# Streamed tiles spaced 64 bytes apart in a pool of their own, a reordered first unit, and last columns in halves

## The chip, the cores and the metric

The kernel runs on one core of a Trainium2 chip. The metric is the device time of one execution in microseconds (us). Three runs of the kernel before gave 2600.47, 2601.5 and 2602.29 us; the median is 2601.5 us.

## The reference

Two decoder layers over 256 tokens of width 2048, all in float32. Each layer adds three things to the residual x: a mixer, a cross-attention and a gated feed-forward block, each behind an RMS norm. The mixer projects the normed x to 6924 columns and runs four attention variants of four heads each side by side.

```python
for layer in range(DEPTH):                       # 2
    h = rms_norm(x, mix_norm[layer])
    proj = h @ w_in[layer]                       # 2048 x 6924
    ...                                          # retention, stick-breaking, hgrn2, nsa
    x = x + mix @ w_out[layer]                   # 2048 x 2048
    x = x + cross_attention(rms_norm(x, ..), rms_norm(mem, ..), ..)
    x = x + conv_ffn(rms_norm(x, ..), ffn_w_up[layer], .., ffn_w_down[layer])   # 2048 x 11264, 5632 x 2048
return rms_norm(x, final_norm)
```

Nearly all the arithmetic is the product of 256 rows of activations with weights that are read once.

## The kernel before, in words

The weights come as 880 units in one fixed list. A unit is a slab of up to 128 x 1024 float32 values: two slices of 128 rows of K by 512 columns (`group_a`), or four slices by 256 columns (`group_b`). For each unit one DMA on SP's queue fills a tile `raw` (`u_dma`, L392), ScalarE copies it into a tile `hi` of the narrower type float32r (`u_hi`, L397), and VectorE writes the remainder raw - hi into a tile `lo` (`u_lo`, through the helper at L247). Activations lie in the same form: `xt_tile` gives a tile of 128 x 2 x 256 whose first half holds the high part (`hi_part`, by `act` at L242 or a copy at L260) and whose second half the low part (`lo_part`, L247 or L250). A tag `xt` holds normed inputs, a tag `mg` the outputs of the attention variants and of the gated block; 16 buffers each.

Every product is three matmuls: high by high, high by low, low by high. `group_a` holds an activation tile stationary and streams 512 columns of weight (L411, L412, L413, moving `hi`, `lo`, `hi`). `group_b` holds 128 weight columns stationary and streams the activation tile: eight matmuls of 512 columns (L476, moving both halves of `xt`, stationary `hi`) and eight of 256 columns (L479, stationary `lo`).

One pool `sb` holds every tile in order of first use. The tags `xt`, `hi` and `lo` follow one another in buffers of 2048 or 4096 bytes per partition, so all their tiles start at the same place within every 512 bytes. Between `lo` and `mg` lie small tiles of 17088 bytes in all, 33 times 512 and 192 more, so each `mg` tile starts 192 bytes further within 512 than a `hi` or `lo` tile.

The main loop walks the units. At unit i it issues the DMA of unit i + 6, does `more(i)` (loads of x, constants and parameters at fixed units), makes `hi` of unit i + 3 and `lo` of unit i + 2, then issues the unit's matmuls and one step of each side chain (`tick`). Before the loop the first six units are loaded, with the four transposed pieces of x (`turned`) in between, and `first_norm` makes the first activation tiles. Each engine works through its instructions in program order.

At the end `group_tail` (L432) computes the last 512 columns: the last three units first for token rows 0 to 127, then for rows 128 to 255, and `last_rows` (L1469) adds each half to x, takes the sum of squares, forms 1/sqrt by `rsqrt` (L497: logarithm, exponential and one Newton step), scales four tiles and stores them from SP's queue (L1491).

Of the kernel before, what the change touches and what calls it, by code (L numbers as in the profile page):

```python
# [133 lines left out]
def shape_consts():  # L134
    f = np.float32
    i = np.arange(128)
    c = {}
    lg = np.log1p(-np.exp2(-5.0 - np.arange(H)))
    rel = (i[None, :] - i[:, None]).astype(np.float64)
    dec = np.zeros((128, H, 2, 128))  # L140
    for h in range(H):
        dec[:, h, 0] = np.where(rel >= 0, np.exp(lg[h] * np.maximum(rel, 0)), 0.0)
        dec[:, h, 1] = np.exp(lg[h] * (rel + 128))
    ident = np.eye(128)
    ones = np.ones((128, 128))
# [12 lines left out]
    inv = (10000.0 ** (-(np.arange(64) / 64))).astype(f)  # L158
    half_pi = np.full((128, 1), np.pi / 2)
    parts = [("ident", ident), ("ones", ones), ("inv", np.broadcast_to(inv, (128, 64))), ("hpi", half_pi),  # L160
             ("tri", tri), ("dec", dec * SCALE), ("sbm", sbm), ("cm", cm),
             ("sel", (i[:, None] % 32 == np.arange(15)[None, :]) * 1.0), ("cadd", np.where(ok, 0.0, NEG)), ("cmul", ok * 1.0)]
# [31 lines left out]
def body(ctx, tc, w, x, xt_in, mem, mem_t, pos, consts, masks, pars, wck, wcv, fnorm, out):  # L194
# [5 lines left out]

    sb = ctx.enter_context(tc.tile_pool(name="sb", bufs=1))
# [3 lines left out]
    count = [0]  # L205

# [16 lines left out]
    def xt_tile(tag):  # L223
        return sb.tile([128, 2, 256], F32R, name=nm(tag), tag=tag, bufs=16)
# [76 lines left out]
    nc.sync.dma_start(par[0][:, 0:16], pars[0, :, 0:16])  # L301
# [10 lines left out]
    def more(i):  # L312

        if i in (1, 3, 5, 7):
            k = i // 2
            for t in range(2):
                nc.sync.dma_start(xs[t][k], x[t * 128:(t + 1) * 128, k * 512:(k + 1) * 512])
        elif i == 6:
# [18 lines left out]
    stage = {}  # L337
# [50 lines left out]

    def u_dma(u):
        n = u.nk * u.cols  # L390
        u.raw = sb.tile([128, n], F32, name=nm("raw"), tag="raw", bufs=AHEAD - LO + 1, padded_shape=[128, 1024])
        nc.sync.dma_start(u.raw, bass.AP(tensor=w.tensor, offset=u.off, ap=[[n, 128], [1, n]]))  # L392

    def u_hi(u):
        n = u.nk * u.cols
        u.hi = sb.tile([128, n], F32R, name=nm("hi"), tag="hi", bufs=HI + 1, padded_shape=[128, 1024])
        A.copy(u.hi, u.raw)  # L397

    def u_lo(u):
        n = u.nk * u.cols  # L400
        u.lo = sb.tile([128, n], F32R, name=nm("lo"), tag="lo", bufs=LO + 1, padded_shape=[128, 1024])
        tt(u.lo, u.raw, f(u.hi), OP.subtract)
        u.raw = None
# [28 lines left out]
    def group_tail(src, klists, n, ends):  # L432
# [3 lines left out]
        late = []  # L436

        def products(u, kl, i, rows):
            for j, k in enumerate(kl):
                mm_a(u, st["ps"], src(k), j, n, i == 0 and j == 0, i == z and j == len(kl) - 1, rows)  # L440

        for i, kl in enumerate(klists):
            def pe(u, i=i, kl=kl):
                if i == 0:
                    st["ps"] = [acc([128, 512]) for _ in range(2)]
                if i < z - LO:
                    products(u, kl, i, (0, 1))
                elif i == z - LO:
                    late.extend((units[u.at + d], klists[i + d], i + d) for d in range(LO + 1))
                    late[:] = [(v, v.hi, v.lo, a, b) for v, a, b in late]  # L450
                    for v, _, _, a, b in late:
                        products(v, a, b, (0,))
                else:
                    for v, hi, lo, a, b in late:
                        v.hi, v.lo = hi, lo
                        products(v, a, b, (1,))
                    del late[:]

            def done(i=i):
                start(ends[i == z](st["ps"][i == z]))  # L460
            unit(pe, done if i in (z - LO, z) else None,
# [179 lines left out]
    def layer(l):  # L641
# [791 lines left out]
        for what, g, k in ffn_order():  # L1433
# [4 lines left out]
            elif what == "down" and g[-1] == tail[-1] and k == 3 and nn is None:  # L1438
                group_tail(gsrc, pairs(g), 512, (last_rows(0), last_rows(1)))
# [9 lines left out]
    def last_chunk(k):  # L1449
        def ev(ps):  # L1450
# [12 lines left out]
            yield  # L1463
# [5 lines left out]
    def last_rows(t):  # L1469

        def ev(ps):
            n = fin["n"]
            tt(xs[t][3], xs[t][3], ps, OP.add)
            n.squares(3, (t,))
            tot = small(1)
            V.tensor_reduce(tot, n.ss[:, t], axis=AX.X, op=OP.add)  # L1476
            steps = rsqrt(tot, 1, 1.0 / D)
            while True:
                try:
                    next(steps)  # L1480
                except StopIteration as e:
                    r = e.value
                    break
            for q in range(4):
                if q % 2 == 0:
                    act(xs[t][q], xs[t][q], AF.Copy, scale=r[:, 0:1])
                elif q == 1:
                    ts(xs[t][q], xs[t][q], r[:, 0:1], None, OP.mult)
                else:
                    stt(xs[t][q], xs[t][q], r[:, 0:1], fin["g"][q], OP.mult, OP.mult)  # L1490
                nc.sync.dma_start(out[t * 128:(t + 1) * 128, q * 512:(q + 1) * 512], xs[t][q])  # L1491
            yield from ()
        return ev
# [12 lines left out]
    def first_norm():  # L1506
        n = NORM[0]
        for k in range(4):
            yield from n.chunk_of(k, xT.pop(k))
        for k in range(4):  # L1510
            yield
# [15 lines left out]
    first = first_norm()  # L1527
    next(first)
    u_hi(units[0])
    u_hi(units[1])  # L1530
    next(first)
    start(first)
    u_hi(units[2])
    for i in range(LO):
        u_lo(units[i])
    for i in range(n):
        if i + AHEAD < n:
            u_dma(units[i + AHEAD])
        more(i)
        if i + HI < n:  # L1540
# [81 lines left out]
```

## Time and profile before

| | |
|---|---|
| Median of three runs | 2601.5 us |
| The profiled execution's own time | 2601.13 us |
| Its span, first to last instruction | 2599.3 us |
| PE (TensorE matmul) busy | 2577.4 us, 99% |
| PEld (weight load) busy | 2211.7 us, 85% |
| DVE (VectorE) busy | 1777.1 us, 68% |
| ACT (ScalarE) busy | 1364.5 us, 52% |
| DMA queue of SP | 54.9% of 16 engines' span |
| Mean granted TensorE clock | 0.999 |

Busy time of PE is not the same as PE at its peak: matmuls are pipelined, and each record reaches from the start of one matmul to a modelled end that lies inside the next one. What a matmul costs in a dense stream is the distance from its start to the start of the next, and that is read from the timeline. A line such as L247 is that of a helper and stands for many places of the program; the tile names tell them apart.

### The profile page before, as it was taken

How to read it: one execution, taken by the hardware profiler on the slowest of the kernel's cores; microseconds unless marked ns; L12 is line 12 of the kernel's file. 1: busy time of each engine (PE TensorE's matmuls, PEld its weight loads, DVE VectorE, ACT ScalarE, POOL GpSimd, SP SyncE). 2: the span in 40 equal slices, each digit the busy share in tenths (PEclk: the TensorE clock that was granted, in tenths of full speed). 3: DMA queues.
4: the chain of work that ended last, by engine and by line, in shares of the span. 5: the costliest groups of instructions: out<-in, count | busy, mean ns of one | idle time of the engine just before them, and what ended most of it. 6: DMA issues, size and time to landing. Idle time of an engine off the chain costs nothing. (4 is left out here: it accounts for less than half of the span.)

```text
span 2599.3 us, 37253 instructions
## 1 busy us (share of the span) xinstructions
PE 2577.4 (99%) x13842; PEld 2211.7 (85%) x13842; DVE 1777.1 (68%) x2877; ACT 1364.5 (52%) x2157; POOL 45.5 (2%) x79
## 2 busy tenths in 40 slices
PE   8999999999999999999999999999999999999998
PEld 7888888888888888888889888889888888888886
DVE  6776665667667676676768666656676766766766
ACT  6545545566455555454555455445654545454554
POOL 0010000000000000000000100000000000000000
PEclk9999999999999999999999999999999999999999
DMA  7564466545555555655555744655455555656654
GB/s 275 180 228 139 153 199 217 188 153 188 188 187 192 189 192 186 193 182 193 186 181 161 227 135 151 205 183 180 159 188 191 189 189 188 191 188 192 205 189 142
DMA packets 136439, 483.66 MB, mean 186 GB/s; under 512 B 15937, under 2 KB 16449, under 8 KB 136257
## 3 DMA queue, kind: packets, MB, share of 16 engines
q1 hardware_dynamic: 131456, 465.55, 54.9%
q0 software_dynamic: 4800, 15.73, 1.9%
q8 instruction: 109, 1.79, 0.3%
q14 instruction: 74, 0.60, 0.1%
HBM read 479.12 MB, written 2.10 MB: 185 GB/s over the span
## 5 line engine op out<-in xcount | busy, mean ns | idle before, releaser
L247 DVE TENSOR_TENSOR lo<-raw,hi 128x1024 fp32r<-128x1024 f32 (+2 forms) x880 | 1067.7, 1214 | 752.6 <-issue 281.3
L397 ACT CAST hi<-raw 128x1024 fp32r<-128x1024 f32 (+2 forms) x880 | 917.8, 1044 | 1174.8 <-PE acc L413 506.2
L476 PE MATMUL acc<-xt,hi 128*128 128x512 f32 x3456 | 870.6, 394 | 9.0 <-ACT hi L397 9.0
L476 PEld LDWEIGHTS acc<-xt,hi 128*128 128x128 f32 x3456 | 623.4, 189 | 125.3 <-ACT hi L397 9.0
L479 PEld LDWEIGHTS acc<-xt,lo 128*128 128x128 f32 x3456 | 471.5, 190 | 33.9
L479 PE MATMUL acc<-xt,lo 128*128 128x256 f32 x3456 | 481.8, 282 | 0.0
L411 PE MATMUL acc<-hi,mg 128*128 128x512 f32 (+1 forms) x1152 | 439.6, 382 | 0.1
L413 PE MATMUL acc<-hi,mg 128*128 128x512 f32 (+1 forms) x1152 | 438.5, 381 | 0.0
L412 PE MATMUL acc<-lo,mg 128*128 128x512 f32 (+1 forms) x1152 | 436.5, 379 | 0.0
L412 PEld LDWEIGHTS acc<-lo,mg 128*128 128x128 f32 x1152 | 216.4, 188 | 42.8
L411 PE MATMUL acc<-hi,xt 128*128 128x512 f32 (+2 forms) x640 | 252.0, 394 | 0.0
L411 PEld LDWEIGHTS acc<-hi,mg 128*128 128x128 f32 x1152 | 216.5, 188 | 41.7 <-ACT mg L260 1.0
L413 PEld LDWEIGHTS acc<-hi,mg 128*128 128x128 f32 x1152 | 216.5, 188 | 40.9 <-DVE mg L247 0.3
L413 PE MATMUL acc<-hi,xt 128*128 128x512 f32 (+2 forms) x640 | 243.2, 380 | 0.0
L412 PE MATMUL acc<-lo,xt 128*128 128x512 f32 (+2 forms) x640 | 242.9, 380 | 0.0
L250 DVE SCALAR_TENSOR_TENSOR s<-s,par,s 128x255 f32<-128x255 f32 x352 | 161.9, 481 | 6.3
L411 PEld LDWEIGHTS acc<-hi,xt 128*128 128x128 f32 x640 | 120.4, 188 | 21.0 <-issue 2.3
L412 PEld LDWEIGHTS acc<-lo,xt 128*128 128x128 f32 x640 | 120.4, 188 | 20.8 <-issue 1.9
L413 PEld LDWEIGHTS acc<-hi,xt 128*128 128x128 f32 x640 | 120.1, 188 | 20.6
L242 ACT ACTIVATE s<-s,par 128x256 f32<-128x256 f32 x176 | 96.0, 593 | 0.6 <-DVE s L247 0.6
L247 DVE TENSOR_TENSOR s<-acc,s 128x256 f32<-128x256 f32 x224 | 83.9, 417 | 0.0
L247 DVE TENSOR_TENSOR x<-x,acc 128x512 f32<-128x512 f32 x128 | 81.9, 681 | 1.9 <-PE acc L413 1.9
(184 smaller groups left out, 1381.6 us busy)
## 6 DMA issues: line engine op xcount, KB each, us to landing
raw<-in_w_dram SPq DMA_DIRECT2D x848, 512.0 KB, 3.5
raw<-in_w_dram SPq DMA_DIRECT2D x16, 396.0 KB, 3.1
raw<-in_w_dram SPq DMA_DIRECT2D x16, 384.0 KB, 3.0
s<-in_nsa_w_ck_dram POOLq DMA_DIRECT2D x16, 256.0 KB, 5.6
s<-in_nsa_w_cv_dram POOLq DMA_DIRECT2D x16, 256.0 KB, 4.6
s<-in_memt_dram POOLq DMA_DIRECT2D x16, 256.0 KB, 5.0
s<-in_xt_dram SPq DMA_DIRECT2D x8, 256.0 KB, 6.4
x<-in_x_dram SPq DMA_DIRECT2D x8, 256.0 KB, 5.9
```

What stands on the lines that cost most here:

```text
L242: A.activation(o, i, func, bias=bias, scale=scale)
L247: V.tensor_tensor(o, a, b, op=op)
L250: V.scalar_tensor_tensor(o, a, s, b, op0=op0, op1=op1)
L397: A.copy(u.hi, u.raw)
L411: T.matmul(ps[t][:, 0:n], lhsT=xh, rhs=hi, start=first, stop=False)
L412: T.matmul(ps[t][:, 0:n], lhsT=xh, rhs=lo, start=False, stop=False)
L413: T.matmul(ps[t][:, 0:n], lhsT=xl, rhs=hi, start=False, stop=last)
L476: T.matmul(st["ps"][q].rearrange("p a b -> p (a b)"), lhsT=u.hi[:, at:at + 128], rhs=xk[kk].rearrange("p a b -> p (a b)"), start=i == 0 an ...
L479: T.matmul(st["ps"][q][:, 1, :], lhsT=u.lo[:, at:at + 128], rhs=xk[kk][:, 0, :], start=False, stop=i == 3 and kk == 3)
```

## The change

Three parts. First, `raw`, `hi`, `lo`, `xt` and `mg` move into a pool `flow` that is opened before `sb`, behind a filler of 1920 bytes; a tile of `hi` or `lo` takes 4160 bytes instead of 4096, one of `xt` or `mg` 2112 instead of 2048. Second, the first loads are put in order of need, the first unit's load, copy and remainder are done in two halves, and two loads go on ScalarE's queue. Third, the last 512 columns are computed in three parts (rows 0 to 127 whole, rows 128 to 255 in two halves of columns), the final scaling of a part is written behind the sum of the next, and `rsqrt` has fewer steps.

```diff
+    flow = ctx.enter_context(tc.tile_pool(name="flow", bufs=1))
     sb = ctx.enter_context(tc.tile_pool(name="sb", bufs=1))
...
+    flow.tile([128, 480], F32, name="edge", tag="edge")
...
     def xt_tile(tag):
-        return sb.tile([128, 2, 256], F32R, name=nm(tag), tag=tag, bufs=16)
+        o = flow.tile([128, 512], F32R, name=nm(tag), tag=tag, bufs=16, padded_shape=[128, 528])
+        return o.rearrange("p (a b) -> p a b", a=2)
...
-    nc.sync.dma_start(par[0][:, 0:16], pars[0, :, 0:16])
+    nc.scalar.dma_start(par[0][:, 0:16], pars[0, :, 0:16])
...
-        if i in (1, 3, 5, 7):
-            k = i // 2
+        if 3 <= i < 7:
+            k = i - 3
             for t in range(2):
                 nc.sync.dma_start(xs[t][k], x[t * 128:(t + 1) * 128, k * 512:(k + 1) * 512])
-        elif i == 6:
+            fetched.append(i)
+        elif i == 7:
...
     def u_dma(u):
         n = u.nk * u.cols
-        u.raw = sb.tile([128, n], F32, name=nm("raw"), tag="raw", bufs=AHEAD - LO + 1, padded_shape=[128, 1024])
-        nc.sync.dma_start(u.raw, bass.AP(tensor=w.tensor, offset=u.off, ap=[[n, 128], [1, n]]))
+        u.raw = flow.tile([128, n], F32, name=nm("raw"), tag="raw", bufs=AHEAD - LO + 1, padded_shape=[128, 1024])
+        for a, b in parts_of(u):
+            q = nc.scalar if u.off == 0 and a == 0 else nc.sync
+            q.dma_start(u.raw[:, a:b], bass.AP(tensor=w.tensor, offset=u.off + a, ap=[[n, 128], [1, b - a]]))
...
-        u.hi = sb.tile([128, n], F32R, name=nm("hi"), tag="hi", bufs=HI + 1, padded_shape=[128, 1024])
-        A.copy(u.hi, u.raw)
+        u.hi = flow.tile([128, n], F32R, name=nm("hi"), tag="hi", bufs=HI + 1, padded_shape=[128, 1040])
+        for a, b in parts_of(u):
+            A.copy(u.hi[:, a:b], u.raw[:, a:b])
...
-    def group_tail(src, klists, n, ends):
+    def group_tail(src, klists, n, end):
...
+        def products(hi, lo, kl, i, p):
             for j, k in enumerate(kl):
+                t, c0, c1 = ((0, 0, n), (1, 0, w), (1, w, n))[p]
...
-    def rsqrt(ms, n, scale):
+    def rsqrt(ms, n, scale, more=None):
         m, y, z = small(n), small(n), small(n)
-        ts(m, ms, scale, EPS, OP.mult, OP.add)
+        more = c("eps") if more is None else more
+        act(y, ms, AF.Ln, scale=scale, bias=more)
+        ts(m, ms, scale, more, OP.mult, OP.add)
+        act(y, y, AF.Exp, scale=-0.5)
+        ts(m, m, -0.5, None, OP.mult)
         yield
-        act(y, m, AF.Ln)
-        act(y, y, AF.Exp, scale=-0.5)
-        yield
-        tt(z, y, y, OP.mult)
-        tt(z, z, m, OP.mult)
-        ts(z, z, -0.5, 1.5, OP.mult, OP.add)
-        tt(y, y, z, OP.mult)
+        if n == 1:
+            stt(z, y, m, y, OP.mult, OP.mult)
+        else:
+            tt(z, y, y, OP.mult)
+            tt(z, z, m, OP.mult)
+        stt(y, z, 1.5, y, OP.add, OP.mult)
         return y
...
+    def last_part(p, ps):
+        t, a, b = ((0, 0, 512), (1, 0, 256), (1, 256, 512))[p]
+        x3 = xs[t][3][:, a:b]
+        tt(x3, x3, ps[:, 0:b - a], OP.add)
+        tot = small(1)
+        act(s_tile([128, b - a]), x3, AF.Square, accum=fin["n"].ss[:, 1, 3:4] if p == 1 else tot)
+        if p != 1:
+            fin["steps", t] = rsqrt(tot, 1, 1.0 / D, fin[t])
+            next(fin["steps", t])
+        if p == 0:
+            tt(x3, x3, fin["g"][3][:, a:b], OP.mult)
+            return
+        if p == 1:
+            last_scale(0)
+            so_far(1, 4)
+        else:
+            last_scale(1)
...
+            (nc.scalar if q in (0, 3) and t == 1 else nc.sync).dma_start(o, xs[t][q])
...
-    for i in range(AHEAD):
-        if i < 4:
-            xT[i] = turned(xt_in, i, nc.sync)
-        u_dma(units[i])
+    xT[0] = turned(xt_in, 0, nc.sync)
+    u_dma(units[0])
+    u_dma(units[1])
+    xT[1] = turned(xt_in, 1, nc.sync)
+    u_dma(units[2])
+    for i in (2, 3):
+        u_dma(units[i + 1])
+        xT[i] = turned(xt_in, i, nc.sync)
+    u_dma(units[5])
     load_table(AF.Exp)
     first = first_norm()
+    first_parts = parts_of(units[0])
...
+    for h, (a, b) in enumerate(first_parts):
+        xk = [xt_tile("xt") for _ in range(2)]
+        for i in range(2):
+            hi_part(xk[i], tiles[h][:, i, :], pc(0, "mix", 2 * h + i))
+        for i in range(2):
+            lo_part(xk[i], tiles[h][:, i, :], pc(0, "mix", 2 * h + i))
+            NORM[0].k[2 * h + i] = xk[i]
+        A.copy(u.hi[:, a:b], u.raw[:, a:b])
+        tt(u.lo[:, a:b], u.raw[:, a:b], f(u.hi[:, a:b]), OP.subtract)
```

## Rows read from the trace of the kernel before

**Rows 1.** Busy time by engine, whole span (us, share, instructions).
```profile
PE 2577.4 (99%) x13842; PEld 2211.7 (85%) x13842; DVE 1777.1 (68%) x2877; ACT 1364.5 (52%) x2157; POOL 45.5 (2%) x79
```
**Rows 2.** Waits of PE: who waited for whom, total us, times, longest.
```profile
PE acc L476 <- ACT hi L397: 9.0, 1, 9.0
```
**Rows 3.** Groups by line and shape, four matmul shapes: count, busy us, mean ns.
```profile
L476 PE MATMUL acc<-xt,hi 128*128 128x512 f32 x3456 | 870.6, 394 | 9.0 <-ACT hi L397 9.0
...
L411 PE MATMUL acc<-hi,mg 128*128 128x512 f32 x1024 | 402.4, 393 | 0.1
...
L411 PE MATMUL acc<-hi,xt 128*128 128x512 f32 x512 | 207.5, 405 | 0.0
```
**Rows 4.** Timeline of PE, first and last of 192 matmuls over xt: start, length.
```profile
55.80 0.40 PE L411 MATMUL acc<-hi,xt 128*128 128x512 f32 x1
...
99.11 0.39 PE L413 MATMUL acc<-hi,xt 128*128 128x512 f32 x1
```
**Rows 5.** Timeline of PE, first and last of 192 matmuls over mg.
```profile
676.34 0.39 PE L411 MATMUL acc<-hi,mg 128*128 128x512 f32 x1
...
720.06 0.39 PE L413 MATMUL acc<-hi,mg 128*128 128x512 f32 x1
```
**Rows 6.** Timeline of PE, first and last of 91 matmuls in the tail.
```profile
2564.40 0.40 PE L411 MATMUL acc<-hi,mg 128*128 128x512 f32 x1
...
2585.40 0.40 PE L411 MATMUL acc<-hi,mg 128*128 128x512 f32 x1
```
**Rows 7.** Timeline of PE, two units of group_b, 25 units apart.
```profile
600.92 2.00 PE L476 MATMUL acc<-xt,hi 128*128 128x512 f32 x8
...
669.80 1.12 PE L479 MATMUL acc<-xt,lo 128*128 128x256 f32 x8
670.75 2.00 PE L476 MATMUL acc<-xt,hi 128*128 128x512 f32 x8
```
**Rows 8.** Timeline of PE, plain float32 matmuls of 256 columns between streams.
```profile
355.77 0.59 PE L1163 MATMUL wk<-s,s 128*128 128x256 f32 x2
356.20 0.38 PE L1164 MATMUL wk<-s,s 128*128 128x128 f32 x2
```
**Rows 9.** Timeline of all engines at the start.
```profile
2.11 0.43 SPq L392 DMA_DIRECT2D raw<-in_w_dram  x1
...
3.92 1.70 ACT L242 ACTIVATE xt<-s,par 128x256 fp32r<-128x256 f32 x4 [1.91 <-DMA s<-in_xt_dram]
...
7.88 1.04 ACT L397 CAST hi<-raw 128x1024 fp32r<-128x1024 f32 x1 [2.25 <-DMA raw<-in_w_dram]
...
8.97 3.70 PE L476 MATMUL acc<-xt,hi 128*128 128x512 f32 x8 [8.97 <-ACT hi L397]
...
12.51 1.12 PE L479 MATMUL acc<-xt,lo 128*128 128x256 f32 x8
...
13.47 2.00 PE L476 MATMUL acc<-xt,hi 128*128 128x512 f32 x8
```
**Rows 10.** Timeline of all engines at the end.
```profile
2589.36 0.39 PE L413 MATMUL acc<-hi,mg 128*128 128x512 f32 x1
2589.45 5.98 SPq L1491 DMA_DIRECT2D out_dram<-x  x8
2589.79 0.69 DVE L247 TENSOR_TENSOR x<-x,acc 128x512 f32<-128x512 f32 x1
2590.51 0.63 ACT L244 ACTIVATE s<-x 128x512 f32<-128x512 f32 x1 [0.48 <-DVE x L247]
...
2591.65 0.44 ACT L242 ACTIVATE m<-m 128x1 f32<-128x1 f32 x2 [0.41 <-DVE m L256]
...
2592.89 1.34 ACT L242 ACTIVATE x<-x,m 128x512 f32<-128x512 f32 x2 [0.81 <-DVE m L247]
2592.89 0.49 DVE L254 TENSOR_SCALAR x<-x,m 128x512 f32<-128x512 f32 x1
2593.29 0.75 DVE L250 SCALAR_TENSOR_TENSOR x<-x,m,s 128x512 f32<-128x512 f32 x1
```

More of the change, by code (lines that the diff above doesn't have):

```diff
@@ L160, in shape_consts @@
     parts = [("ident", ident), ("ones", ones), ("inv", np.broadcast_to(inv, (128, 64))), ("hpi", half_pi),
+             ("eps", np.full((128, 1), EPS)),
              ("tri", tri), ("dec", dec * SCALE), ("sbm", sbm), ("cm", cm),
@@ L335, in more @@
             nc.sync.dma_start(par[1], pars[1])
-    stage = {}
+    stage, fetched, now = {}, [], [0]
     def pc(l, n, i):
@@ L436, in group_tail @@
         late = []
-        def products(u, kl, i, rows):
+        w = n // 2
+        def products(hi, lo, kl, i, p):
             for j, k in enumerate(kl):
-                mm_a(u, st["ps"], src(k), j, n, i == 0 and j == 0, i == z and j == len(kl) - 1, rows)
+                xk = src(k)
+                a, b = i == 0 and j == 0, i == z and j == len(kl) - 1
+                t, c0, c1 = ((0, 0, n), (1, 0, w), (1, w, n))[p]
+                xh, xl = (xk[:, q, t * 128:(t + 1) * 128] for q in range(2))
+                o = st["ps"][p][:, 0:c1 - c0]
+                T.matmul(o, lhsT=xh, rhs=hi[:, j * n + c0:j * n + c1], start=a, stop=False)
+                T.matmul(o, lhsT=xh, rhs=lo[:, j * n + c0:j * n + c1], start=False, stop=False)
+                T.matmul(o, lhsT=xl, rhs=hi[:, j * n + c0:j * n + c1], start=False, stop=b)
         for i, kl in enumerate(klists):
@@ L444, in pe @@
                 if i == 0:
-                    st["ps"] = [acc([128, 512]) for _ in range(2)]
+                    st["ps"] = [acc([128, 512]), acc([128, 512]), wk([128, 512])]
                 if i < z - LO:
-                    products(u, kl, i, (0, 1))
+                    for p in range(3):
+                        products(u.hi, u.lo, kl, i, p)
                 elif i == z - LO:
[L449 to L456, printed above, removed]
+                    late.extend((units[u.at + d].hi, units[u.at + d].lo, klists[i + d], i + d) for d in range(LO + 1))
+                    for p in range(3):
+                        for v in late:
+                            products(*v, p)
+                        end(p, st["ps"][p])
                     del late[:]
-            def done(i=i):
-                start(ends[i == z](st["ps"][i == z]))
-            unit(pe, done if i in (z - LO, z) else None,
+            unit(pe, None,
                  lambda i=i: tuple(src(k) for kl in (klists if i >= z - LO else klists[:i + 1]) for k in kl))
@@ L1438, in layer @@
             elif what == "down" and g[-1] == tail[-1] and k == 3 and nn is None:
-                group_tail(gsrc, pairs(g), 512, (last_rows(0), last_rows(1)))
+                group_tail(gsrc, pairs(g), 512, last_part)
             elif what == "down":
@@ L1462, in ev @@
                 tt(xs[t][k], xs[t][k], ps[t], OP.add)
-            yield
+            if k < 2:
+                yield
             n.squares(k)
@@ L1466, in ev @@
                 tt(xs[t][k], xs[t][k], fin["g"][k], OP.mult)
-        return ev
[L1469 to L1493, printed above, removed]
+            if k == 2:
+                so_far(0, 3)
@@ new lines, in last_chunk, with so_far @@
+        return ev
+    def so_far(t, k):
+        fin[t] = small(1)
+        V.tensor_reduce(fin[t], fin["n"].ss[:, t, 0:k], axis=AX.X, op=OP.add)
+        ts(fin[t], fin[t], 1.0 / D, EPS, OP.mult, OP.add)
+    def last_part(p, ps):
[15 more added lines that the diff above has]
+            last_scale(1)
@@ new lines, in last_scale @@
+    def last_scale(t):
+        try:
+            next(fin["steps", t])
+        except StopIteration as e:
+            r = e.value
+        for q in (1, 0, 2, 3):
+            o = out[t * 128:(t + 1) * 128, q * 512:(q + 1) * 512]
+            if q == 0 or t == 0 and q == 2:
+                act(xs[t][q], xs[t][q], AF.Copy, scale=r[:, 0:1])
+            elif t == 1 and q == 3:
+                stt(xs[t][q], xs[t][q], r[:, 0:1], fin["g"][q], OP.mult, OP.mult)
+            else:
+                ts(xs[t][q], xs[t][q], r[:, 0:1], None, OP.mult)
+            (nc.scalar if q in (0, 3) and t == 1 else nc.sync).dma_start(o, xs[t][q])
@@ L1507, in first_norm @@
         n = NORM[0]
-        for k in range(4):
+        for k in range(1, 4):
             yield from n.chunk_of(k, xT.pop(k))
         for k in range(4):
-            yield
+            while len(fetched) <= k or now[0] < fetched[k] + 2:
+                yield
             n.squares(k)
@@ L1521, in body @@
     n = len(units)
-    for i in range(AHEAD):
-        if i < 4:
-            xT[i] = turned(xt_in, i, nc.sync)
-        u_dma(units[i])
+    xT[0] = turned(xt_in, 0, nc.sync)
[7 more added lines that the diff above has]
+    u_dma(units[5])
     load_table(AF.Exp)
     first = first_norm()
+    first_parts = parts_of(units[0])
+    u = units[0]
+    u.hi = flow.tile([128, 1024], F32R, name=nm("hi"), tag="hi", bufs=HI + 1, padded_shape=[128, 1040])
+    u.lo = flow.tile([128, 1024], F32R, name=nm("lo"), tag="lo", bufs=LO + 1, padded_shape=[128, 1040])
+    tiles = xT.pop(0)
+    for h, (a, b) in enumerate(first_parts):
[6 more added lines that the diff above has]
+        A.copy(u.hi[:, a:b], u.raw[:, a:b])
+        tt(u.lo[:, a:b], u.raw[:, a:b], f(u.hi[:, a:b]), OP.subtract)
+    u.raw = None
+    u_hi(units[1])
+    u_lo(units[1])
     next(first)
-    u_hi(units[0])
-    u_hi(units[1])
+    u_hi(units[2])
     next(first)
     start(first)
-    u_hi(units[2])
-    for i in range(LO):
-        u_lo(units[i])
     for i in range(n):
@@ L1539, in body @@
         more(i)
+        now[0] = i
         if i + HI < n:
```

7 lines of the change are left out of this document (5 added, 2 removed).

## The prediction

> **What bounds the kernel now.** I read the busy time by engine first. TensorE is busy for 99% of the span and no other engine for more than 68% (its weight loads, which run beside the matmuls, 85%) [rows 1], so a change is worth what it takes off TensorE's own stream, or off the two ends where that stream does not run. Its waits come next: 9.0 us at the start [rows 2]. Behind its last matmul lie 9.55 us [rows 10]. The span without these two is 2580.7 us, and TensorE is busy for 2577.4 of it, so all holes in the middle come to 3.3 us. What is left is the pace of the stream, and that is read from the timeline as the distance between starts. There the reader is to see that one instruction, a float32r matmul of 512 columns, has no single price:
>
> - over `xt` tiles, (99.11 - 55.80)/191 = 0.2268 us [rows 4];
> - over `mg` tiles, (720.06 - 676.34)/191 = 0.2289 us [rows 5];
> - over `mg` tiles in the last 21 us, (2585.40 - 2564.40)/90 = 0.2333 us [rows 6].
>
> The first two are the same three lines of code with the same shapes. The moving tiles are the same too. What differs is where the stationary tile lies: `xt` at the same place within 512 bytes as `hi` and `lo`, `mg` 192 bytes further. So the pace depends on how the two operands lie to each other. The third has the same layout as the second and another pace, so it also depends on how the stream was started (it follows a short stall). A unit of `group_b` takes (670.75 - 600.92)/25 = 2.793 us, of which the eight matmuls of 256 columns take 670.75 - 669.80 = 0.95 us, or 0.119 each, and the eight of 512 columns the other 1.84, or 0.230 each [rows 7].
>
> **The change, part by part.**
>
> *The spacing.* Number of matmuls of 512 columns [rows 3]: L476 over `xt` 3456 and over `mg` 128 (the rest of that line's 448 units), L411 to L413 over `mg` 3 x 1024 and over `xt` 3 x 512. Together 8192, at a mean of (3584 x 0.230 + 3072 x 0.2289 + 1536 x 0.2268)/8192 = 0.2290 us, 1876 us of the span. After the change every tile of these tags starts on a multiple of 64 bytes, and neighbours of a tag lie 64 bytes apart within 512, so the relation of moving to stationary goes through eight values instead of two. The trace shows two of these values, and neither of them is wrong by itself, so the price must be bounded:
>
> - all 8192 at the pace of `xt`: 8192 x (0.2290 - 0.2268) = 18 us less;
> - all at the pace of the tail: 8192 x (0.2333 - 0.2290) = 35 us more;
> - the far end: plain float32 matmuls of 256 columns, which stream at half the rate, go by at (356.20 - 355.77)/2 = 0.215 us each [rows 8]. That is as long as 512 columns at full rate would be without the excess. All 8192 at 0.215 would be 115 us less.
>
> The nearest rows are the first two. I take the value that lies nearest to them: the `mg` streams, whose relation is the poor one now, come to the pace of `xt`, 3072 x 0.0021 = 6.5 us less, and L476 and `xt` keep theirs, since a good relation that is lost in some tiles is found in others. The matmuls of 256 columns I leave at 0.119. The copies into `hi` and the remainders on DVE and ACT may shift by a few ns with the offsets; both engines have idle time enough (68% and 52% busy [rows 1]).
>
> The Trainium skill speaks against this term. Its page "SBUF — State Buffer", section "SBUF: two separate sides", says that the engines' ports do not contend apart from the pair that VectorE and GpSimd share: "PE, ACT, and DVE's dedicated pair never wait on anyone." By that rule the place of a tile would not matter, the term would be zero and the sum that of the two ends alone. The rows [rows 4, 5] differ by 2.1 ns a matmul where only the place of one operand differs, so I hold the rule as a rival and not as the forecast.
>
> *The first unit.* TensorE starts at 8.97 when the first `hi` is there; that copy began at 7.88 when the raw tile had landed, though the first activation pieces were there at 3.92, and the second unit started at 13.47 [rows 9]. After the change the first raw half (256 KB) goes on ScalarE's queue beside the first activations and ahead of everything else, instead of 512 KB issued at 2.11 behind them. Halves of the casts cost ACT 2 x 0.43 for the first two activation slices (1.70/4 each) and about 0.55 for half a copy, so if the half lands by 4.8 TensorE starts near 5.4 to 6.0. The first eight matmuls took 12.51 - 8.97 = 3.54 us, far slower than the later 1.84, and I let them stay as slow. They end near 9.2, and the eight of L479 at 10.2, so the second unit begins about 3 us earlier: 3.0 us less. What is late next is the second unit: its raw tile, now third in SP's queue, its cast (1.04 us) and its remainder must be done by 10.4. Bounds: no gain if the first half still lands at 7.88; 4 us if it lands with the activations. The two DMAs on ScalarE's queue are issued ahead of the table load, 0.4 us each, and are hidden while ACT waits for the activations until 3.92. The first copy on ACT now waits for its half with the second pair of activation casts, the second half and unit 1's copy queued behind it. TensorE alone waits for those. The loads of x move from units 1, 3, 5 and 7 to 3 to 6, and the constants from 6 to 7; they pass only raw loads of units 7 to 13 on SP's queue, and their use (the norm's sums) comes behind unit 8, ahead of any matmul that needs the norm. I cost them at nothing.
>
> *The last columns.* The last matmul starts at 2589.36 and ends about 2589.75. Then come the addition 0.69, the square 0.63 and its read-out, the sum over four, the logarithm and exponential 0.44, four small DVE steps, and the factor is there at 2592.89. DVE then takes 0.49 and 0.75, ACT 1.34, and SP issues its last store until 2589.45 + 5.98 = 2595.43; the execution's span ends at 2599.3 [rows 10]. So the last matmul lies 9.55 us from the end. After the change the last part is 256 columns wide: addition and square each fall by about 0.25 and 0.2, the sum over four is gone, the Newton step is two instructions instead of four (0.2 each), and the read of the mean is folded into the logarithm. The factor comes 1.85 us behind the last matmul instead of 3.14. Against this, rows 0 to 127's scaling is now in the queue ahead of the last addition. It starts when the second part's 18 matmuls are done, 2.1 us before the end, and takes DVE some 2.4 us, so the last addition waits about 0.3. DVE then has three scalings (0.4, 0.49, 0.75) instead of two and ACT one; the stores of the last rows leave on two queues, the last at +4.3 instead of +5.68. That is 1.4 us less. The 24 matmuls of 512 columns for rows 128 to 255 become 48 of 256 in the three parts: 48 x 0.119 - 24 x 0.2333 = 0.1 us more. I take 1.2 us less, with bounds of zero (if draining 2 MB of stores sets the end) and 2.5.
>
> *rsqrt elsewhere.* A shorter chain of small instructions in the norms and heads; all of TensorE's holes in the middle come to 3.3 us, so I cost it at nothing.
>
> *Sum.* The profiled execution took 2601.13 us, 1.83 more than its span, and lies 0.4 below the median of the runs. 2601.1 - 6.5 - 3.0 - 1.2 = 2590.4, say 2590 us.
>
> **The rivals.**
>
> 1. *The spacing does nothing*, as the rule above has it, or good and poor relations cancel. For it: the two layouts shown differ by only 1%. Against it: they do differ, at the same instructions. The ends alone pay: 2601.1 - 4.2 = 2597 us.
> 2. *A much better pace.* If most of the excess over 0.215 comes from both operands being read from the same place of the memory at the same time, then spreading the relation cuts into the excess itself. For it: the half-rate streams have none [rows 8]. Against it: the two relations shown share most of it. Half of the excess gone: 8192 x 0.007 = 57 us less, 2540 us.
> 3. *The slow pace becomes common*, and the time is longer. Now 192 matmuls in a row repeat one relation and settle at one pace; with tiles at eight relations every new tile pair disturbs the stream, and rows 6 show that a disturbed stream can stay at 0.2333. The place is L476 and L411 to L413, the price up to 35 us: 2601.1 + 35 - 4.2 = 2632 us. It decides from a mean of 0.2290 + 4.2/8192 = 0.2295 us upward, half a nanosecond, where the ends' gain is used up.
>
> **How the numbers follow.** Chances: the forecast 0.40 (2577 to 2600 by its own bounds of 18 and 0 us for the spacing and 1 to 6.5 for the ends); rival 1 0.20; rival 2 0.16; rival 3 0.24. The range: down to 2542, which nearly reaches the whole of rival 2, and up to 2615, which takes in half of rival 3. About 8% lie below and 10% above. A measurement of this kernel tells about 0.2%, 5.2 us, from no change, so faster means under 2596.3. The forecast gives 0.38 of that, rival 2 its 0.16, rival 1 0.05: 0.59. Same: rival 1 0.14, the forecast 0.02 and rival 3's lower end 0.02: 0.18. Slower: 0.23.
>
> **What would show it.** For the spacing: the distance between starts in the long streams of `mg` should fall from 0.2289 to about 0.227, in those of `xt` and in the unit of `group_b` (2.793) stay; all paces above 0.2295 mean rival 3, paces below 0.224 rival 2. For the first unit: the first matmul near 5.7 and the second unit near 10.5 instead of 13.47. For the end: the span's end 8.3 instead of 9.55 us behind the last matmul. I am wrong if the middle, from the third unit to the last stream, changes by more than 18 us either way.

## The result, and the profile after

The change made the kernel slower by half a per cent: 2614.77 us median (four runs, 2614.73 to 2614.97) against 2600.98 us for the kernel before (four runs), a ratio of 1.0053 with a 95% interval of 1.0039 to 1.0067. The forecast was 2590 us and faster.

The profiled execution took 2614.97 us, its span is 2613.2. First the page's line of busy time, which answers to [rows 1]:

```profile
PE 2594.5 (99%) x13866; PEld 2212.7 (85%) x13866; DVE 1779.3 (68%) x2881; ACT 1363.1 (52%) x2158; POOL 45.4 (2%) x79
```

TensorE is busy for 17.1 us more and no other engine for more than 2.2, so nothing was added beside the stream: the stream itself is longer. The waits of PE (who waited for whom, total us, times, longest) hold no new entry of any size; the one at the start has shrunk against [rows 2]:

```profile
PE acc L494 <- ACT hi L1585: 7.0, 1, 7.0
...
PE acc L462 <- DVE lo L251: 0.2, 1, 0.2
```

Three distances make up the span. From its start to the first matmul 8.97 us became 7.02; from the first matmul's start to the last one's 2580.39 became 2597.42; from there to the span's end 9.94 became 8.76. That is -1.95 + 17.03 - 1.18 = +13.9 us, the whole change of the span (2599.3 to 2613.2). The loss lies between the first and the last matmul, and the timeline of PE shows what it is (start, length). These rows answer to [rows 4, 5, 7]:

```profile
54.25 0.40 PE L425 MATMUL acc<-hi,xt 128*128 128x512 f32 x1
...
98.33 0.39 PE L427 MATMUL acc<-hi,xt 128*128 128x512 f32 x1
...
600.68 2.02 PE L494 MATMUL acc<-xt,hi 128*128 128x512 f32 x8
...
669.80 1.13 PE L497 MATMUL acc<-xt,lo 128*128 128x256 f32 x8
670.76 2.01 PE L494 MATMUL acc<-xt,hi 128*128 128x512 f32 x8
...
679.15 0.39 PE L425 MATMUL acc<-hi,mg 128*128 128x512 f32 x1
...
723.41 0.39 PE L427 MATMUL acc<-hi,mg 128*128 128x512 f32 x1
```

- 192 matmuls over `xt`: (98.33 - 54.25)/191 = 0.2308 us each, before 0.2268;
- 192 over `mg`: (723.41 - 679.15)/191 = 0.2317, before 0.2289;
- 25 units of `group_b`: (670.76 - 600.68)/25 = 2.803 us, before 2.793.

No stretch that I measured runs at 0.2268 any more. The groups by line and shape (count, busy us, mean ns) tell the same, beside [rows 3]:

```profile
L494 PE MATMUL acc<-xt,hi 128*128 128x512 f32 x3456 | 875.1, 395 | 7.0 <-ACT hi L1585 7.0
L425 PE MATMUL acc<-hi,mg 128*128 128x512 f32 x1008 | 399.4, 396 | 0.1
```

394 ns became 395 and 393 became 396. These means reach to a modelled end inside the next matmul, so I go by distances between starts, taken over the whole trace with those above 0.26 us (waits) left out. Mean us, before and after:

| matmul | count | before | after | us |
|---|---|---|---|---|
| `group_a`, 512 columns, `mg` | 3016 | 0.2292 | 0.2314 | +6.6 |
| `group_a`, 512 columns, `xt` | 1466 | 0.2279 | 0.2310 | +4.6 |
| `group_b`, 512 columns, `xt` | 3417 | 0.2301 | 0.2315 | +4.6 |
| `group_b`, 256 columns, `xt` | 3456 | 0.1192 | 0.1189 | -0.9 |

That is 14.9 of the 17.0 us. Both ends of the kernel did move about as intended. The timeline of all engines shows it (start, length), at the start in answer to [rows 9] and at the end to [rows 10]:

```profile
1.17 0.45 ACTq L404 DMA_DIRECT2D raw<-in_w_dram  x1
...
3.73 0.91 ACT L246 ACTIVATE xt<-s,par 128x256 fp32r<-128x256 f32 x2 [0.79 <-DMA par<-in_pars_dram]
...
6.35 0.62 ACT L1585 CAST hi<-raw 128x512 fp32r<-128x512 f32 x1 [1.72 <-DMA raw<-in_w_dram]
...
7.02 3.78 PE L494 MATMUL acc<-xt,hi 128*128 128x512 f32 x8 [7.02 <-ACT hi L1585]
...
10.60 1.34 PE L497 MATMUL acc<-xt,lo 128*128 128x256 f32 x8
...
11.78 2.02 PE L494 MATMUL acc<-xt,hi 128*128 128x512 f32 x8
...
2604.17 3.92 SPq L1532 DMA_DIRECT2D out_dram<-x  x6
...
2604.44 0.28 PE L463 MATMUL wk<-hi,mg 128*128 128x256 f32 x1
...
2604.76 0.42 DVE L251 TENSOR_TENSOR x<-x,wk 128x256 f32<-128x256 f32 x1
2605.21 0.42 ACT L248 ACTIVATE s<-x 128x256 f32<-128x256 f32 x1
...
2606.77 0.88 DVE L258 TENSOR_SCALAR x<-x,m 128x512 f32<-128x512 f32 x2
2607.52 1.18 ACTq L1532 DMA_DIRECT2D out_dram<-x  x2
2607.56 0.75 DVE L254 SCALAR_TENSOR_TENSOR x<-x,m,s 128x512 f32<-128x512 f32 x1
```

The first raw half landed only at 6.35: ScalarE waited 1.72 us for it. In both kernels the first matmuls run at the lower of the clock's two levels. They start 0.427 us apart, which for 512 columns is 1.2 GHz, and the trace's record of the granted clock rises to full speed at 12.46 us before and at 11.11 us after, when TensorE had worked since 8.97 and since 7.02. So the rise came 1.35 us earlier, the first matmul 1.95. At the end the last addition is 0.42 long instead of 0.69, the factor is there 2.33 us behind the last matmul's start (2606.77 - 2604.44) instead of 3.53, and SP's last store is issued at 2608.09.

### The profile page after: what moved, and what is told of

Its sections match the earlier page's. It is cut to its first block, busy times and chain, and to the rows that moved or that the text cites. A ratio compares the mean times of both kernels' runs of the same rounds, so it can differ in the third digit from the quotient of the medians.

```text
span 2613.2 us, 37308 instructions
## 1 busy us (share of the span) xinstructions
PE 2594.5 (99%) x13866; PEld 2212.7 (85%) x13866; DVE 1779.3 (68%) x2881; ACT 1363.1 (52%) x2158; POOL 45.4 (2%) x79
## 5 line engine op out<-in xcount | busy, mean ns | idle before, releaser
L251 DVE TENSOR_TENSOR lo<-raw,hi 128x1024 fp32r<-128x1024 f32 (+3 forms) x881 | 1067.6, 1213 | 762.3 <-issue 272.7
L425 PE MATMUL acc<-hi,mg 128*128 128x512 f32 (+1 forms) x1136 | 436.9, 385 | 0.1
L427 PE MATMUL acc<-hi,mg 128*128 128x512 f32 (+1 forms) x1136 | 432.4, 381 | 0.0
L427 PEld LDWEIGHTS acc<-hi,mg 128*128 128x128 f32 x1136 | 213.4, 188 | 44.3 <-DVE mg L251 0.3
L425 PEld LDWEIGHTS acc<-hi,mg 128*128 128x128 f32 x1136 | 213.4, 188 | 43.1 <-ACT mg L264 1.0
```

The source lines that it names most:

```text
L251: V.tensor_tensor(o, a, b, op=op)
L425: T.matmul(ps[t][:, 0:n], lhsT=xh, rhs=hi, start=first, stop=False)
L427: T.matmul(ps[t][:, 0:n], lhsT=xl, rhs=hi, start=False, stop=last)
```

## The experiments

The distance of two tiles below is the start of the moving tile minus that of the stationary one, within 256 bytes. In `group_a` the weight moves and the activation is stationary, in `group_b` the other way round. So a tag that lies 64 bytes behind the weights is at distance 64 in `group_b` and at 192 in `group_a`.

My theory (A) was that the tile-to-tile change of the distance keeps the stream from settling: a distance that stays settles at its own pace, one that changes with each tile does not. Rivals: (B) the new order of the loads and the split first unit disturb the stream; (C) the new pool's place in memory does, without the 64 bytes; (D) the pace of the `mg` streams has nothing to do with their distance. The tables of paces have been read in the same way for every kernel.

**1. Both ends alone.** The changed kernel, with all tiles back in `sb` and no spacing.

```diff
-    flow = ctx.enter_context(tc.tile_pool(name="flow", bufs=1))
+    flow = sb
-    flow.tile([128, 480], F32, name="edge", tag="edge")
-        o = flow.tile([128, 512], F32R, name=nm(tag), tag=tag, bufs=16, padded_shape=[128, 528])
+        o = flow.tile([128, 512], F32R, name=nm(tag), tag=tag, bufs=16, padded_shape=[128, 512])
```
(and 1024 for 1040 in `hi` and `lo`)

> The change without its spacing: the first unit, the last columns and rsqrt as changed, all tiles back in one pool with their old sizes (xt, hi and lo at one place within 512 bytes, mg 192 further). Theory A (the varied places of the tiles slow TensorE's stream): the two ends keep their gain, 2.1 us at the first matmul and 1.0 behind the last, and the middle goes back to that of the kernel before, so 2598 us. Theory B (the reordered loads or the new queue order slow the middle): 2615 us, as the change. Pace over mg: A 0.2289 us, B above 0.231.

Measured: 2598.38 us, ratio 0.9990 (0.9981 to 0.9998); paces as before (0.2291 over `mg`, 0.2278 over `xt`, 0.2301 in `group_b`). The ends gain 2.7 us, and B falls.

**2. The spacing alone.** The kernel before, with the pool `flow` and the 64 bytes, nothing else.

```diff
+    flow = ctx.enter_context(tc.tile_pool(name="flow", bufs=1))
+    flow.tile([128, 480], F32, name="edge", tag="edge")
-        return sb.tile([128, 2, 256], F32R, name=nm(tag), tag=tag, bufs=16)
+        o = flow.tile([128, 512], F32R, name=nm(tag), tag=tag, bufs=16, padded_shape=[128, 528])
+        return o.rearrange("p (a b) -> p a b", a=2)
```
(and `raw`, `hi`, `lo` from `flow`, the last two padded to 1040)

> The kernel before with the pool of spaced tiles alone, old order at both ends. Theory A (the varied places slow the stream): the middle takes 17 us longer, 2618 us, and the paces over xt and mg are both about 0.231. Theory B (the order of loads does it): 2601 us, paces 0.2268 and 0.2289.

Measured: 2616.52 us, ratio 1.0058 (1.0044 to 1.0071). Its timeline over the first 192 `mg` matmuls:

```profile
681.50 0.40 PE L414 MATMUL acc<-hi,mg 128*128 128x512 f32 x1
...
725.63 0.40 PE L416 MATMUL acc<-hi,mg 128*128 128x512 f32 x1
```

(725.63 - 681.50)/191 = 0.2310: the slow stream is all here, without the new ends.

**3. The whole change without the 64 bytes.** The pool stays; every tile now starts at the same place within 256 bytes.

```diff
-        o = flow.tile([128, 512], F32R, name=nm(tag), tag=tag, bufs=16, padded_shape=[128, 528])
+        o = flow.tile([128, 512], F32R, name=nm(tag), tag=tag, bufs=16, padded_shape=[128, 512])
-        u.hi = flow.tile([128, n], F32R, name=nm("hi"), tag="hi", bufs=HI + 1, padded_shape=[128, 1040])
+        u.hi = flow.tile([128, n], F32R, name=nm("hi"), tag="hi", bufs=HI + 1, padded_shape=[128, 1024])
```
(`lo` likewise)

> The change with its own pool at the same place, but without the 64 bytes between tiles: hi, lo, xt and mg all start at multiples of 512. Theory A (what costs is that the relation of moving to stationary tile changes from tile to tile): one relation for all streams, that of xt before, so xt and mg both at 0.2268; 2601.0 - 3.1 - 6.5 = 2591 us. Theory C (the new pool or the starts at multiples of 64 cost, whatever the spacing): 2615 us, paces at 0.231.

Measured: 2594.13 us, ratio 0.9971 (0.9960 to 0.9981), 20.6 us below the changed kernel. The page's line of busy time:

```profile
PE 2574.0 (99%) x13866; PEld 2215.7 (85%) x13866; DVE 1778.9 (69%) x2881; ACT 1365.8 (53%) x2158; POOL 45.2 (2%) x79
```

and the timeline of PE over the same `mg` stretch:

```profile
675.17 0.40 PE L425 MATMUL acc<-hi,mg 128*128 128x512 f32 x1
...
718.49 0.39 PE L427 MATMUL acc<-hi,mg 128*128 128x512 f32 x1
```

(718.49 - 675.17)/191 = 0.2268. TensorE has the same 13866 matmuls and is busy for 20.5 us less. By groups, the 64 bytes add 12.9 us over `mg`, 4.9 over `xt` in `group_a` and 5.0 in the 512-column matmuls of `group_b`, and take off 2.5 in those of 256 columns: 20.3 us, beside the 20.2 measured between first and last matmul. C falls: pool, filler and order are the same here. A's 2591 us is missed by 3 us: the ends gain 2.7 us instead of 3.1, and the 256-column matmuls over `mg` lose 2.2 us against experiment 1.

**4. The kernel before with `mg` moved onto the weights' place.** A filler of 320 bytes, so that 192 become 512.

```diff
+        if tag == "mg" and not gap:
+            gap.append(sb.tile([128, 80], F32, name="gap", tag="gap"))
```

> The kernel before with a filler of 320 bytes ahead of the mg tiles, so that these too start at the place of hi and lo within 512 bytes; nothing else. Theory A (a fixed relation lets the stream settle, and the relation 0 settles at the lower pace): mg falls from 0.2289 to 0.2268, 3072 x 2.1 ns less, 2594.5 us. Theory D (any fixed relation is as good, and xt and mg differ for another reason): 2601 us, mg stays at 0.2289.

Measured: 2597.10 us, ratio 0.9983 (0.9974 to 0.9992). Its timeline of PE over the first 192 `mg` matmuls:

```profile
677.14 0.40 PE L413 MATMUL acc<-hi,mg 128*128 128x512 f32 x1
...
720.46 0.39 PE L415 MATMUL acc<-hi,mg 128*128 128x512 f32 x1
```

(720.46 - 677.14)/191 = 0.2268: D falls, and what the forecast wanted of `mg` is had by a filler. The `mg` matmuls of 512 columns gain 6.3 us, but between first and last matmul it is only 3.7, since those of 256 columns lose 2.8 (2.0 over `mg`, from 0.1166 to 0.1203 in `group_a` and 0.1141 to 0.1191 in `group_b`, and 0.7 over `xt`). I had priced 256 columns as one figure.

**5 and 6. Other fixed distances.** Experiment 3 with one filler ahead of the first `xt` tile and one ahead of the first `mg` tile. Two theories stood open: each distance has its own pace (A1), or any fixed distance settles at 0.227 (A2).

```diff
+        if tag not in gaps:
+            gaps[tag] = PLACE[tag]
+            if gaps[tag]:
+                flow.tile([128, gaps[tag] // 4], F32, name="gap" + tag, tag="gap" + tag)
...
+PLACE = {"xt": 64, "mg": 64}       # xt 64, mg 128 bytes behind the weights' place
+PLACE = {"xt": 192, "mg": 64}      # xt 192, mg 256
```
(one of the last two lines in each kernel; the comments are not in the code)

> The unspaced version (all relations fixed) with a filler ahead of xt and of mg, so that xt lies 64 and mg 128 bytes behind hi and lo within 512. Theory A1 (each fixed relation has its own settled pace): two new paces between 0.2268 and 0.2333. Theory A2 (any fixed relation settles at 0.227, only variation costs): both 0.227, 2594 us.

> As before with xt at 192 and mg at 256. Theory A1: xt now has the relation that mg had before the change, so streams over xt come to 0.2289 and the eight matmuls of L476 to about 0.233 as those over mg had; mg between 0.2268 and 0.2333; 2594 + 1536 x 2 ns + 3456 x 3 ns = 2607 us or more. Theory A2: 0.227 for both, 2594 us.

Measured: `xt` 64 and `mg` 128: 2604.77 us, ratio 1.0015 (1.0005 to 1.0026), with 0.2333 over `xt` and 0.2326 over `mg` in `group_a`. `xt` 192 and `mg` 256: 2589.61 us, ratio 0.9955 (0.9939 to 0.9971). A2 falls: the paces run from 0.2270 to 0.2333. The second time is a miss. Its 512-column paces came as A1 has them, 0.2292 for `xt` in `group_a` and 0.2328 in `group_b`, a loss of 11.4 us against experiment 3, but the 256-column matmuls fell from 0.1194 to 0.1145, and 3456 of them gave 17 us back.

A1 is right only on the mean, for one distance can hold two paces. These are the first and the last matmul of two streams of 192 over `mg` in the first of the two kernels, both at distance 128:

```profile
678.54 0.40 PE L429 MATMUL acc<-hi,mg 128*128 128x512 f32 x1
...
723.11 0.39 PE L431 MATMUL acc<-hi,mg 128*128 128x512 f32 x1
...
811.60 0.39 PE L429 MATMUL acc<-hi,mg 128*128 128x512 f32 x1
...
855.99 0.40 PE L431 MATMUL acc<-hi,mg 128*128 128x512 f32 x1
```

(723.11 - 678.54)/191 = 0.2334 and (855.99 - 811.60)/191 = 0.2324. The kernel before does the same at distance 64, with 0.2289 in its streams over `mg` and 0.2333 in its tail [rows 5, 6]. Which of the two a stream takes, no run here settles.

**7 and 8. Which tiles' spacing counts.** The changed kernel with the 64 bytes kept for `hi` and `lo` alone, and for `xt` and `mg` alone.

```diff
 # weights only
-        o = flow.tile([128, 512], F32R, name=nm(tag), tag=tag, bufs=16, padded_shape=[128, 528])
+        o = flow.tile([128, 512], F32R, name=nm(tag), tag=tag, bufs=16, padded_shape=[128, 512])
 # activations only
-        u.hi = flow.tile([128, n], F32R, name=nm("hi"), tag="hi", bufs=HI + 1, padded_shape=[128, 1040])
+        u.hi = flow.tile([128, n], F32R, name=nm("hi"), tag="hi", bufs=HI + 1, padded_shape=[128, 1024])
```
(`lo` likewise)

> The change with the 64 bytes kept for hi and lo alone, xt and mg unspaced. Theory A (a stream pays when the relation changes from one matmul to the next): in L425 to L427 hi and lo alternate, and now lie at different places, so these streams stay near 0.231; in group_b a unit's eight matmuls of 512 columns keep one relation and settle, nearer to 0.230. About 2607 us. Rival (the spacing of the activations is what costs): 2594 us, paces of 0.227 over xt and mg.

> The change with the 64 bytes kept for xt and mg alone, hi and lo unspaced. Theory A: group_b meets a new relation every two matmuls and stays near 0.2315, group_a keeps one activation tile for six matmuls and comes to some 0.229 to 0.230. About 2606 us. Rival (the spacing of the weights is what costs): 2594 us, paces of 0.227 over xt and mg.

Measured: 2609.45 us, ratio 1.0031 (1.0019 to 1.0044), and 2607.81 us, ratio 1.0027 (1.0016 to 1.0037). Either half alone costs 15.3 and 13.7 us against experiment 3, both together 20.6, so they do not add up. In `group_a` each half alone already brings the whole loss (0.2312 with spaced weights, 0.2316 to 0.2318 with spaced activations). In `group_b` they differ: 0.2314 with spaced weights, but 0.2288 with spaced activations, below the 0.2300 of no spacing at all. Both rivals fall, and the two times came near A's, but of A's four paces only one did (`group_a` with spaced weights). With spaced weights a unit of `group_b` keeps its distance for eight matmuls and should have come nearer to 0.230; with spaced activations `group_a` keeps it for six and should have come to 0.229 to 0.230, and `group_b` should have stayed near 0.2315. That last figure I cannot explain: the four slices of a unit then lie at four distances, and the mean of the four fixed paces (table below) would be 0.2311.

**9 and 10. What the distance repeats by.** The fillers of 5 and 6 with two more settings.

```diff
+PLACE = {"xt": 320, "mg": 64}      # xt 320, mg 384
+PLACE = {"xt": 128, "mg": 128}     # xt 128, mg 256
```

> All xt tiles start 320 bytes and all mg tiles 384 bytes after the weight tiles, counted within 512 bytes (64 and 128 plus 256); no 64-byte spacing. If the pace of a matmul goes by the distance between moving and stationary tile within 256 bytes, this is the kernel with 64 and 128 again: streams over xt 0.2333 us, over mg 0.2326 us, 512-column matmuls of the projection units 0.2291 us, 256-column ones 0.1162 us, 2604.8 us. If it goes by 512 bytes or by where in memory a tile lies, these four numbers differ from those by more than 0.001 us and the time by more than 5 us.

> All xt tiles start 128 bytes and all mg tiles 256 bytes after the weight tiles; no 64-byte spacing. If the pace goes by the distance moving minus stationary within 256 bytes alone, streams over xt take what streams over mg took at 128 (0.2326 us), streams over mg 0.2271 us, and the 512-column matmuls of the projection units 0.2326 us (their distance is minus 128, the same). The 256-column ones at this distance were not seen yet: between 0.1145 and 0.1194 us, so that the time is between 2593 and 2611 us. If the two roles are not mirrored so, the 512-column matmuls of the projection units come out elsewhere.

Measured: `xt` 320 and `mg` 384: 2604.76 us, ratio 1.0016 (1.0007 to 1.0025), with 0.2333, 0.2326, 0.2291 and 0.1162, the four paces of 64 and 128 again. So the pace repeats by 256 bytes. Nor does it go by where the tiles lie: by the program's addresses the weight tiles of experiment 4 start 224 bytes past a multiple of 256 and those of experiment 3 on a multiple, and with all distances at 0 both have 0.2271 over `mg` and 0.2300 to 0.2301 in `group_b`. `xt` 128 and `mg` 256: 2607.71 us, ratio 1.0025 (1.0015 to 1.0035); 0.2324 over `xt`, 0.2270 over `mg`, 0.2326 in `group_b`, as expected, and 0.1189 for 256 columns.

**11. The fastest one again.**

> The kernel with xt 192 and mg 256 bytes after the weight tiles again, in five rounds beside the kernel before: 2589.6 us, ratio 0.9955. If its gain over the unspaced kernel (2594.1 us) lies in the 256-column matmuls, these again take 0.1145 us on the mean against 0.1194 us there. If the first look was chance, it comes back to 2594 us or more.

Measured: 2589.24 us, ratio 0.9954 (0.9940 to 0.9968), 25.5 us under the changed kernel and 11.9 under the one before it. Its timeline of PE over units of `group_b`:

```profile
600.12 2.02 PE L498 MATMUL acc<-xt,hi 128*128 128x512 f32 x8
...
668.54 1.07 PE L501 MATMUL acc<-xt,lo 128*128 128x256 f32 x8
669.45 2.02 PE L498 MATMUL acc<-xt,hi 128*128 128x512 f32 x8
```

and the group of its 256-column matmuls (count, busy us, mean ns):

```profile
L501 PE MATMUL acc<-xt,lo 128*128 128x256 f32 x3456 | 465.7, 277 | 0.0
```

A unit takes (669.45 - 600.12)/25 = 2.773 us, and its eight matmuls of 256 columns (669.45 - 668.54)/8 = 0.114.

Put together, mean distance between starts in us, by the distance of the tiles (moving minus stationary, within 256 bytes) where it is the same for all tiles of a tag:

| distance | 512, `group_a` | 512, `group_b` | 256 |
|---|---|---|---|
| 0 | 0.2270 to 0.2279 | 0.2299 to 0.2303 | 0.1190 to 0.1203 |
| 64 | 0.2292 | 0.2291 | 0.1162 to 0.1166 |
| 128 | 0.2324 to 0.2326 | 0.2326 to 0.2327 | 0.1189 to 0.1192 |
| 192 | 0.2333 | 0.2328 to 0.2329 | 0.1141 to 0.1146 |
| changes (after) | 0.2310 to 0.2314 | 0.2315 | 0.1183 to 0.1189 |

The `xt` and `mg` tiles, and the two roles, fall on the same row as soon as they have the same distance. The last row lies between the best and the worst of a column, above distance 0 and 64 for 512 columns. How much of that is just the mean of good and poor distances shows in the changed kernel itself, grouped by the addresses that the tiles have in the program. Mean distance between starts of its 512-column matmuls, in us:

| distance in the changed kernel | 0 | 64 | 128 | 192 |
|---|---|---|---|---|
| `group_a` | 0.2313 | 0.2308 | 0.2316 | 0.2314 |
| `group_b` | 0.2301 | 0.2301 | 0.2326 | 0.2330 |

In `group_b` these are nearly the paces of the fixed distances again. The mean of the four fixed paces is 0.2311, and 0.2315 was measured: there the loss is in the main the mean, and theory A adds little. In `group_a`, where `hi` and `lo` alternate, the four are alike, and 0 and 64 have lost their low paces, as A has it. But the four fixed paces have a mean of 0.2305 there, against 0.2288 before and 0.2313 after, so about two thirds of the loss is that mean, and the rest goes with the change of distance. Together it is about 11 of the 15.8 us that the table of the result shows for 512 columns. So A1's map stands, and A is the smaller part of the loss. For `group_b` with spaced activations (experiment 8) it stays open what pace a changing distance gives. Why 0.227 and not 0.2333 goes with a distance, no run here shows.

## Why the prediction was wrong

**The spacing** is the step that failed: "the `mg` streams, whose relation is the poor one now, come to the pace of `xt`, 3072 x 0.0021 = 6.5 us less, and L476 and `xt` keep theirs, since a good relation that is lost in some tiles is found in others." The first half was right of the relation: moving `mg` onto the weights' place brings 0.2268 (experiment 4). But the change does not do that. It gives `mg` eight places within 512 bytes, which are four distances within 256, and the same to `xt`. The second half failed: in `group_a` the relations in use before, 0 for `xt` and 64 for `mg`, were the two best of the four, and the tiles that left them found 0.2325 and 0.2333. On top of that, a distance that changes brings `group_a` to 0.231 even at 0 and 64. With the 64 bytes `mg` went to 0.2314, `xt` to 0.2310 and `group_b` to 0.2315. Measured against the kernel with both ends alone (2598.38), the own pool with all tiles at one place is worth -4.3 us and the 64 bytes on top +20.6, so the term is +16.4 where I had -6.5. Its bounds (-18 and +35) held; the value taken between them had the wrong sign. The time lies inside the stated range, by 0.2 us of its upper end: that end had been set to take in half of rival 3, so this is no merit of the forecast.

I could have seen a warning where I averaged. The row of the tail, at the layout of `mg` but another pace [rows 6], showed that the pace depends on what came before, which speaks for a stream that settles. I used it for a rival alone. At distance 0 the same tail goes at 0.2270 (experiment 4), so its slow pace was not that of every disturbed stream.

**Rival 3** came true in its sign, and in part in its mechanism, that every new tile pair disturbs the stream: the larger part of the loss is the mean of good and poor distances. Its point of decision, a mean of 0.2295, is passed; the three rows of 512 columns in the table of the result have a mean of 0.2314 after and 0.2293 before. Its price was too high by half, since I let all stay at the tail's 0.2333: +17 us between first and last matmul instead of up to +35. The sign by which I would call myself wrong, over 18 us in the middle, was not reached (from the third unit's start to the last matmul 2573.1 became 2589.9, +16.8), but "all paces above 0.2295" was.

**Rival 1**, that the place of a tile does not matter, falls. The rule behind it, in the Trainium skill, page "SBUF — State Buffer", section "SBUF: two separate sides", is that TensorE never waits on anyone; experiment 3 and the changed kernel have the same instructions and differ by 20.6 us, and the fixed distances by up to 6 ns in 227. The rule speaks of one engine against another; here it is the place of TensorE's own two operands that decides, and what they meet is not shown. **Rival 2** falls as well: none of the four distances, held fixed, brought 512 columns under a mean of 0.2270, so nothing more of the excess over 0.215 was to be had by them.

**256 columns** I left at 0.119, and in the sum that was right (-0.9 us). But it hid what was to be gained, and the trace of before had it. Its units of `group_b` over `mg`, at a distance of 192:

```profile
501.15 2.02 PE L476 MATMUL acc<-mg,hi 128*128 128x512 f32 x8
503.01 1.07 PE L479 MATMUL acc<-mg,lo 128*128 128x256 f32 x8
503.92 2.02 PE L476 MATMUL acc<-mg,hi 128*128 128x512 f32 x8
```

A unit takes 503.92 - 501.15 = 2.77 us, against 2.793 over `xt` [rows 7], and its 256-column half 0.91 against 0.95. That is the unit of experiment 11, in the sixteen units that I set aside as "the rest of that line's 448".

**The first unit**: forecast 3.0 less, measured 1.7 at the second unit (13.47 to 11.78). The mechanism was right, and two terms were off. I let the first half land by 4.8, and it landed near 6.35, though it was issued at 1.17 instead of 2.11 and is half as large. Beside it the first activations, the second half and unit 1's slab were under way, issued by SP from 0.74 to 2.54; whether these held it back was not tried. The first eight matmuls took 10.60 - 7.02 = 3.58 us, as slow as before, as I had let them. But the eight of 256 columns behind them took 1.18 instead of 0.96, since the clock rose only within them, at 11.11. Both terms vary: over the ten traces with this start the half was there between 5.08 and 6.35, the latest here, and the second unit began between 10.58 and 11.92. In experiment 1 the first matmul started at 6.43, but all eight of 256 columns still ran at the lower clock, 0.213 us apart, and the second unit began at 11.71.

**The last columns**: forecast 1.2 less, measured 1.2. The last addition started 0.32 us behind the start of the last matmul (before 0.43), so the 0.3 that I had put there for the scaling of rows 0 to 127 hardly showed; the factor came 2.33 us behind the start of the last matmul, and ACT's and SP's last issues end at 2608.70 and 2608.09. The first unit and the last columns together measured 2.7 us (experiment 1), against 4.2.

**rsqrt** at nothing: no wait of PE of more than 0.7 us has come into the middle, so no cost or gain of it is to be seen.

## What to carry to other kernels

Where TensorE's own stream is the bound, read its pace as the distance between starts and split it by the tiles that feed it: two streams of the same shape with different paces are a question of where their operands lie. Keep that relation the same from tile to tile and choose it, with one filler per tag; spreading tiles over many places averages away the good relation. Price each shape apart, and then the unit as a whole: the place that is best for 512 columns in `group_a` (0) is among the worst for 256, and for a unit of `group_b` distance 64, the best for its 512 columns and the second best for its 256, is the best of the four (8 x (0.2291 + 0.1162) = 2.762 us, against 2.778 at 192 and 2.794 at 0).

## What the runs showed of the hardware

- The mean pace of a float32r matmul goes with the distance of its two tiles within 256 bytes: 512 columns 0.2270 to 0.2333 us, 256 columns 0.1141 to 0.1203, and 320 and 384 bytes give the same four paces as 64 and 128 to within 0.1 ns.
- The two shapes prefer different distances: at 192 instead of 0, 512 columns in `group_b` lose 2.8 ns each and 256 columns gain 4.9.
- A distance does not set the pace alone: streams over `mg` at 128 go at 0.2324 or at 0.2334 in one kernel, and at 64 the kernel before has 0.2289 in the long streams and 0.2333 in the tail.
- A distance that changes keeps 512 columns in `group_a` at 0.231, above what the same distances give when they stay at 0 or 64; in `group_b` of the changed kernel each distance keeps nearly its own pace (0.2301 to 0.2330).
- The 256-column pace goes also with the 512-column matmuls ahead of it. In the kernel of experiment 7, 34 units of `group_b` have `hi` at distance 64 and `lo` at 192; they took 0.2295 and 0.1181, not the 0.2291 and 0.1145 that the two distances have by themselves, while 30 units with both at 192 took 0.2330 and 0.1148. Distances change from unit to unit there; a kernel that keeps `lo` 128 bytes off `hi` throughout was not tried.
